# Masking the decay rows first, two visits for the gate products, and later key products in a hybrid decoder layer

## The chip, the cores and the metric

The kernel runs on one core of a Trainium2 chip. The metric is device time in microseconds (us) of one execution; lower is better. The core has a matrix engine (TensorE, PE in the profile, with its weight loads as PEld), a vector engine (VectorE, DVE), an engine for activation functions (ScalarE, ACT), a general engine (GpSimd, POOL) and one that here only issues transfers (SyncE, SP). Each engine takes its instructions in its own order and waits for the others by semaphores. Products land in PSUM, eight banks of 128 x 512 floats; all else lives in SBUF or, for longer, in DRAM.

## The reference

One layer of a decoder over 1024 tokens of width 1024, in float32, without a batch:

- x is normalised (RMSNorm), and one projection gives the columns of two mixers.
- Mixer A has four heads of width 128 with a gated delta rule. Queries, keys and values go through a causal convolution of four taps and SiLU; queries and keys are normalised. Each token and head has a step size beta and a log decay g.
- Mixer B is dilated window attention with eight heads of width 64.
- Both outputs go through a projection and are added to x; then comes a normalisation, a gated MLP of inner width 2816 with a convolution of three taps, and a last normalisation.

The part that matters here is the decays and the keys' products of mixer A. In the reference, with gc the running sum of g within a chunk:

```
diff = gc[..., :, None] - gc[..., None, :]
dec_incl = jnp.where(incl, jnp.exp(jnp.where(incl, diff, 0.0)), 0.0)
kk = jnp.einsum('nbhtd,nbhjd->nbhtj', kc, kc)
lmat = dec_strict * kk * bc[..., None, :]
attn = dec_incl * jnp.einsum('nbhtd,nbhjd->nbhtj', qc, kc) * bc[..., None, :]
```

So a head needs the matrix of decays exp(gc_t - gc_j) where t is not before j, and zero elsewhere. The kernel uses chunks of 128 tokens, eight of them (`NCH`).

## The kernel before

**The weave.** The order of work on PE is not written out by hand. Every part of the layer is a generator (`norms`, `gates`, `first`, `dense`, `kprep`, `qprep`, `vprep`, `merge`, `chain`, `attention`, `mlp_up`, ...), added to a planner `Weave` with a level. The planner keeps its own clock of PE and of each engine with a cost per operation; `Weave.run` always resumes the generator of lowest level among those that are due. A generator yields the time until it wants to be resumed: `yield wv.need(tiles, slack=s)` means "when these tiles are ready by the plan, and s us after". `next_bank(tag, *tiles, slack=0.0)` yields until the tiles are ready and a bank of that tag is free by the plan, and then takes the bank; each tag has two banks in turn. The order in which the products are emitted is binding for PE (`stamp_issue_order_token`), and the planner's times are only estimates: on the chip, PE waits wherever its next product's inputs or bank are not there. For the other engines the compiler's scheduler puts the operations in order, by its own estimates, within the dependencies; `after` adds an order between two operations of it.

**Dense products.** The projection's products are the stream that fills PE: `dense` goes over the columns in 128s, for each of them two halves of 512 tokens, and for each half eight times three products (`mm3`: a float32 product is made of three products of parts `hi` and `lo`). In the profile these are `ps<-xhi,wlo`, `ps<-xhi,whi` and `ps<-xlo,whi`. The text counts positions on PE in these dense products from the start of the program. The first three keys come from `first`, which runs while x is being loaded. The weights of a column are loaded to `wst` and split by ACT (`whi`) and DVE (`wlo`).

**Norms and gates.** `norms` sums the squares of x over the channels (eight small products with `ones`), makes `rst` with DVE and POOL, transposes it in two times four transposes into a PSUM bank each, and copies each to `rstdB`. `gates` makes the eight gate rows (beta and decay of four heads) by products of the weights `wba` with x: per half of the tokens eight products in two visits of four, `APART` (0.5 us) apart in the plan. Then come eight products with `sel` that bring the rows to tokens, elementwise work on DVE and ACT, and the running sum by two products with `tri`; the rows of sums go by DMA to DRAM (`gdram`).

**Key preparation, `kprep(h)`, one per head.** First the decay matrix `dec`: the head's rows of sums are loaded from `gdram` into all partitions, ACT subtracts the token's own sum chunk by chunk (eight Identity operations with the bias `ngc`), POOL's `affine_select` writes `NEG` (-1e30) where the mask is off, and ACT takes one Exp over 128 x 1024. A copy `gel` of the last columns is made by DVE before; it overlaps the same tile, so the eight operations on ACT come after it. Two `after` calls put these behind the head's convolution work. Then `tokens` transposes the key chunks: two banks of four transposes (`ps<-ident,kT`), copied to `ktok` by ACT, with eight Squares of 128 x 128 on ACT (`sq<-ps`) that sum the norm to `ssk`. From that DVE and POOL make the scales `nk`, `bp` and `ke`. Then two banks of four key products `ps<-kT` (keys with keys), each followed by four DVE operations `um<-ps,bp,dec` that scale and mask. The four transposes' banks and the products' banks are the same two, of tag `atr`; a product must wait until ACT's last Square has read the bank.

**After the keys.** `qprep(h)` starts when the head's key work is emitted: transposes (`ps<-ident,qT`), eight Squares on ACT, eight products (`ps<-qT,kT`) and eight DVE operations to `at`, in the same banks. `forward_sub` starts after the fourth head's keys; its blocks come through DRAM (`mdram`), DVE inverts, and `merge` builds the inverses by small products (`ps<-x,um` is the first of them) with copies such as `w2` between. Then come the chains over the chunks, attention, the output projection and the MLP, which takes most of the time.

Line numbers: products are recorded at L177, transposes at L181, all operations of ACT, DVE, POOL and the transfers of SP at L132. The work can so be told apart by tile names only.

Of the kernel before, what the change touches and what calls it, by code (L numbers as in the profile page):

```python
# [9 lines left out]
AF = mybir.ActivationFunctionType  # L10
OP = mybir.AluOpType
# [4 lines left out]
P = 128  # L16
# [3 lines left out]
NCH = 8  # L20
FT = 22
NEG = -1.0e30
APART = 0.5
EPS = 1e-6
SLOTS = {"kT": 2, "kU": 2, "dv": 2, "dw": 2, "kt": 4, "uy": 5, "qa": 4, "ev": 2, "go": 2, "Xa": 7, "Xb": 9}
TURNS = {"kT*": ("kT", "kU"), "dv*": ("dv", "dw"), "X": ("Xa",) * 7 + ("Xb",) * 9}
# [109 lines left out]
def hybrid_layer(tc, I, out):  # L136
    nc = tc.nc
    wv = Weave()
    ve = Engine(wv, nc.vector, "vector", 0.07, 0.00105)
    ac = Engine(wv, nc.scalar, "scalar", 0.12, 0.00085)  # L140
    po_ = Engine(wv, nc.gpsimd, "gpsimd", 0.15, 0.0021)
# [69 lines left out]
    def rsqrt(dst, src, n):  # L211
        po_.tensor_tensor(dst, src, mhalf[:, :n], op=OP.pow)
# [13 lines left out]
    def bank(tag, name="ps"):  # L226
        return tile_(pp_, (P, 512), F32, name, tag, 2)

    def next_bank(tag, *tiles, slack=0.0):

        while max(wv.need(*tiles), wv.slot_free(tag, 2)) + slack > 1e-3:
            yield max(wv.need(*tiles), wv.slot_free(tag, 2)) + slack
        return bank(tag)
# [4 lines left out]
    def v8(t):  # L238
        return t.rearrange("p (c t) -> p c t", c=NCH)
# [14 lines left out]
    for k in range(KT):  # L254
# [30 lines left out]
        else:  # L285
            inst = ve.tensor_tensor(acc, acc, sq, op=OP.add)
# [44 lines left out]
    rstdB = const("rstdB", [P, S])  # L331

    def norms():
        yield wv.need(acc, slack=8.0)
        ssp = yield from next_bank("atr", acc)
        for c in range(NCH):
            mm(ssp[:, c:c + 1], acc[:, c * P:(c + 1) * P], ones[:, :1], 0.215)
            if c % 2:
                yield APART
        ve.tensor_scalar(rst, ssp[:, :NCH], 1.0 / 1024, EPS, op0=OP.mult, op1=OP.add)  # L340
        rsqrt(rst, rst, NCH)
        wv.done.add("rst")
        yield wv.need(rst)
        for h in range(2):
            pb = yield from next_bank("atr")
            for c in range(4):
                i = 4 * h + c
                tp(pb[:, c * P:(c + 1) * P], rst[:, i:i + 1].to_broadcast([P, P]))
            ve.tensor_copy(rstdB[:, half(h)], pb)
        wv.done.add("norms")  # L350
# [4 lines left out]
    ngc = sp.tile([P, NCH, H], F32, name="ngc")  # L355

    def gates():

        yield wv.need(wba, xts[-1], slack=4.0)
        for h in range(2):  # L360
            pt = yield from next_bank("atr", wba, xts[-1])
            for k in range(KT):
                o = 32 * (k % 4)
                mm(pt[o:o + 32], wba[:, k, :], xts[k][:, half(h)], 0.23, k < 4, k >= 4, tile_position=(0, o))
                if k == 3:
                    yield APART
            ac.activation(barow[:, half(h)], pt, AF.Copy)
            yield APART
        yield wv.need(barow, slack=2.0)
        pt = yield from next_bank("atr", barow)  # L370
        for c in range(NCH):
            mm(pt[:, c * 8:(c + 1) * 8], barow[:, c * P:(c + 1) * P], sel, 0.215)
            if c % 2:
                yield APART
        yield from wv.until("rst")
        ba = sp.tile([P, NCH, 8], F32, name="ba")
        ve.tensor_tensor(ba, pt[:, :64].rearrange("p (c j) -> p c j", c=NCH),
                                rst[:, :, None].to_broadcast([P, NCH, 8]), op=OP.mult)
        ac.activation(beta, ba[:, :, :H], AF.Exp, scale=-1.0)
        ve.tensor_scalar(beta, beta, 1.0, None, op0=OP.add)  # L380
        ve.reciprocal(beta, beta)
        zt = sp.tile([P, NCH, H], F32, name="zt")
        ve.tensor_tensor(zt, ba[:, :, H:], dtb[:, None, :].to_broadcast([P, NCH, H]), op=OP.add)
        az = sp.tile([P, NCH, H], F32, name="az")
        ac.activation(az, zt, AF.Abs)
        ac.activation(az, az, AF.Exp, scale=-1.0)
        ac.activation(az, az, AF.Ln, bias=1.0)
        ve.scalar_tensor_tensor(az, zt, 0.0, az, op0=OP.max, op1=OP.add)
        ea = sp.tile([P, H], F32, name="ea")
        ac.activation(ea, alog, AF.Exp)  # L390
        g = sp.tile([P, NCH, H], F32, name="g")
        ve.scalar_tensor_tensor(g, az, -1.0, ea[:, None, :].to_broadcast([P, NCH, H]), op0=OP.mult,
                                       op1=OP.mult)
        pt = yield from next_bank("atr", g)
        g32 = g.rearrange("p c h -> p (c h)")
        mm(pt[:, :NCH * H], tri, g32, 0.215)
        mm(pt[:NCH * H, P:2 * P], g32, tri, 0.215)
        grow = tile_(sp, [NCH * H, P], F32, "grow", "osq", 1)
        ac.activation(grow, pt[:NCH * H, P:2 * P], AF.Copy)
        sy.dma_start(gdram, grow)  # L400
        ve.tensor_copy(gc, pt[:, :NCH * H].rearrange("p (c h) -> p c h", c=NCH))
        ve.tensor_scalar(ngc, gc, -1.0, None, op0=OP.mult)
        ac.activation(ngam, gc, AF.Exp)
        ve.tensor_scalar(ngam, ngam, -1.0, None, op0=OP.mult)
        wv.done.add("gates")
# [118 lines left out]
    def kprep(h):  # L524
        d = G[h]
        kT = T["k", h]
        yield from wv.until("gates")
        yield wv.need(gc)

        dec = A("dec", ("dv", "dw")[h % 2])  # L530
        gend = small("gend")
        gel = small("gel")
        rows = gdram.rearrange("(c h) t -> h c t", h=H)[h]
        sy.dma_start(v8(dec), bass.AP(tensor=rows.tensor, offset=rows.offset, ap=[[0, P]] + list(rows.ap)))
        late = "the rows may come later than the keys"
        after(ve.tensor_copy(gel, v8(dec)[:, :, P - 1]), kends[h][1], late)
        for c in range(NCH):
            inst = ac.activation(v8(dec)[:, c, :], v8(dec)[:, c, :], AF.Identity, bias=ngc[:, c, h:h + 1])
            after(inst, kends[h][0], late)
        po_.affine_select(v8(dec), v8(dec), pattern=[[0, NCH], [1, P]], compare_op=OP.is_ge, fill=NEG,  # L540
                                base=0, channel_multiplier=-1)
        ve.tensor_tensor(gend, gel, gc[:, :, h], op=OP.subtract)
        ac.activation(dec, dec, AF.Exp)
        eg = small("eg")
        ac.activation(eg, gend, AF.Exp)
        ge = small("ge", 4)
        ac.activation(ge, gel, AF.Exp)
        yield wv.need(kT, slack=SLACK)
        ssk = small("ssk")
        d["ktok"] = yield from tokens(kT, A("ktok", "kt"), None, ssk)  # L550
        ve.tensor_scalar(ssk, ssk, 4.0 * EPS, None, op0=OP.add)
        nk = small("nk", 4)
        po_.tensor_tensor(nk, ssk, phalf, op=OP.pow)
        bp = small("bp", 4)
        ve.reciprocal(bp, ssk)
        ve.tensor_tensor(bp, bp, beta[:, :, h], op=OP.mult)
        ke = small("ke", 4)
        ve.tensor_tensor(ke, bp, eg, op=OP.mult)

        um = A("um", "uy", shape=(P, NCH, P))  # L560
        for c0 in range(0, NCH, 4):
            pt = yield from next_bank("atr")
            for c in range(4):
                cs = slice((c0 + c) * P, (c0 + c + 1) * P)
                mm(pt[:, c * P:(c + 1) * P], kT[:, cs], kT[:, cs], 0.215)
            for c in range(4):
                i = c0 + c
                ve.scalar_tensor_tensor(um[:, i, :], pt[:, c * P:(c + 1) * P], bp[:, i:i + 1],
                                               dec[:, i * P:(i + 1) * P], op0=OP.mult, op1=OP.mult)
        md = mdram[h].rearrange("(c r) (j i) -> r j c i", r=4, j=32)  # L570
        for r in range(4):
            b = slice(32 * r, 32 * r + 32)
            sy.dma_start(md[r], um[b, :, b])
        d.update(kT=kT, dec=dec, ge=ge, nk=nk, bp=bp, ke=ke, um=um)
        wv.done.add(("k", h))
        if all(("k", i) in wv.done for i in range(H)):
            forward_sub()

    def qprep(h, qT):
# [4 lines left out]
        yield from tokens(qT, None, None, ssq)  # L584
        ve.tensor_scalar(ssq, ssq, 128.0, 128.0 * EPS, op0=OP.mult, op1=OP.add)
        rq = small("rq", 4)
# [143 lines left out]
    def chain(h):  # L730
# [62 lines left out]

        ve.tensor_scalar(ms, ms, 1.0 / 128, EPS, op0=OP.mult, op1=OP.add)
        rsqrt(ms, ms, NCH)
# [290 lines left out]
    def rms2_power():  # L1086
# [3 lines left out]
        rs = sp.tile([P, NCH], F32, name="rs")  # L1090
        ve.tensor_scalar(rs, ps[:, :NCH], 1.0 / 1024, EPS, op0=OP.mult, op1=OP.add)
        rsqrt(rs, rs, NCH)
# [393 lines left out]
```

## Time and profile before

| | us |
|---|---|
| median of 3 runs | 1257.34 |
| lowest and highest run | 1256.65, 1259.51 |
| the profiled execution's own time | 1259.56 |
| its span, first to last instruction | 1257.8 |
| PE busy (98% of the span) | 1233.0 |
| DVE busy (74%) | 936.0 |
| ACT busy (49%) | 621.8 |
| POOL busy (4%) | 47.8 |
| mean granted clock of TensorE | 0.993 |

The span is cut into stretches by the transfers and by the stage: the load of x and the first keys up to about 60 us, key preparation of the four heads between 60 and 115 us, queries, values and the merge up to about 240 us. In a line of the timeline, the first number is the start in us from the span's start, the second the duration of the group of instructions, then come the engine, the line, the operation, the tiles (out<-in), the shape and the number of instructions; in brackets stands how long the engine was idle before and which instruction released it. Matmuls are pipelined, so a group's duration reaches past the start of the next. A line of PE's waits gives what was waited for: total us, times, longest. A line of a table by windows gives the stretch, its length and then for each engine busy us and number of instructions; the last three numbers are the granted clock of PE, the share of the DMA engines and GB/s.

Not only idle time counts: at a granted clock of 0.50 a dense product starts every 0.43 us, and at 1.00 every 0.227 us.

### The profile page before, as it was taken

How to read it: one execution, taken by the hardware profiler on the slowest of the kernel's cores; microseconds unless marked ns; L12 is line 12 of the kernel's file. 1: busy time of each engine (PE TensorE's matmuls, PEld its weight loads, DVE VectorE, ACT ScalarE, POOL GpSimd, SP SyncE). 2: the span in 40 equal slices, each digit the busy share in tenths (PEclk: the TensorE clock that was granted, in tenths of full speed). 3: DMA queues.
4: the chain of work that ended last, by engine and by line, in shares of the span. 5: the costliest groups of instructions: out<-in, count | busy, mean ns of one | idle time of the engine just before them, and what ended most of it. 6: DMA issues, size and time to landing. Idle time of an engine off the chain costs nothing.

```text
span 1257.8 us, 18320 instructions
## 1 busy us (share of the span) xinstructions
PE 1233.0 (98%) x7040; PEld 1002.1 (80%) x7040; DVE 936.0 (74%) x1462; ACT 621.8 (49%) x1179; POOL 47.8 (4%) x34
## 2 busy tenths in 40 slices
PE   9989999999999999999999999999999999999996
PEld 7768887888676767878788888888888888787886
DVE  7566975563555455676798888888988989899875
ACT  7374444462757374465554454544544454343451
POOL 0021110022000000000000000000000000000000
PEclk9989999999999999999999999999999999999998
DMA  6313244255223420454312313223223298545523
GB/s 228 100 57 94 85 116 137 101 160 206 96 78 100 140 63 26 126 179 139 118 51 101 92 59 101 85 67 101 79 73 101 68 353 290 167 138 198 192 85 134
DMA packets 81974, 153.52 MB, mean 122 GB/s; under 512 B 21824, under 2 KB 32736, under 8 KB 81888
## 3 DMA queue, kind: packets, MB, share of 16 engines
q1 hardware_dynamic: 81888, 152.37, 37.1%
q8 instruction: 55, 0.90, 0.3%
q14 instruction: 31, 0.25, 0.1%
HBM read 114.31 MB, written 35.93 MB: 119 GB/s over the span
## 4 chain that ended last, share of the span: by engine, by line
PE 84%; DVE 7%; DMA 4%; ACT 2%; issue 2%; SPq 0%; POOL 0%; POOLq 0%; DVEq 0%; ACTq 0%
PE ps L177 44%; PE pa L177 18%; PE pc L177 9%; PE dw L177 8%; PE ps L181 4%; DMA wd<-in_wd 3%; DVE pr L132 2%; DVE x1h L132 1%; DVE wd L132 1%; ACT dec L132 1%; DVE kT L132 1%; PE warm L177 1%; DMA wst<-in_wu 0%; DVE r L132 0%; DVE xr L132 0%
## 5 line engine op out<-in xcount | busy, mean ns | idle before, releaser
L177 PE MATMUL dw<-pr 128*128 128x512 f32 (+1 forms) x984 | 213.3, 377 | 2.8 <-DVE x1h L132 2.8
L177 PEld LDWEIGHTS dw<-pr 128*128 128x128 f32 x984 | 176.1, 188 | 38.9 <-DVE x1h L132 4.9
L177 PE MATMUL ps<-xhi,whi 128*128 128x512 f32 x448 | 186.5, 416 | 0.0
L177 PE MATMUL ps<-xhi,wlo 128*128 128x512 f32 x448 | 175.8, 392 | 0.0
L177 PE MATMUL ps<-xlo,whi 128*128 128x512 f32 x448 | 175.3, 391 | 0.0
L177 PE MATMUL pa<-T,pair 128*128 128x512 f32 x528 | 127.1, 389 | 0.6 <-ACT u L132 0.6
L177 PEld LDWEIGHTS pa<-T,pair 128*128 128x128 f32 x528 | 99.0, 188 | 21.1 <-ACT u L132 0.7
L177 PEld LDWEIGHTS ps<-xhi,whi 128*128 128x128 f32 x448 | 84.6, 189 | 19.9 <-issue 6.0
L177 PEld LDWEIGHTS ps<-xhi,wlo 128*128 128x128 f32 x448 | 84.4, 188 | 18.5
L177 PEld LDWEIGHTS ps<-xlo,whi 128*128 128x128 f32 x448 | 84.8, 189 | 13.5
L132 ACT ACTIVATE sm<-sm,mx 128x512 f32<-128x512 f32 (+2 forms) x128 | 79.9, 651 | 23.0 <-DVE mx L132 23.0
L132 ACT ACTIVATE u<-pa 128x512 f32<-128x512 f32 x44 | 26.4, 600 | 110.5 <-PE pa L177 110.5
L132 DVE SCALAR_TENSOR_TENSOR y<-xu,fcw,y 128x1023 f32<-128x1023 f32 (+1 forms) x44 | 56.3, 1281 | 25.7 <-ACT y L132 25.7
L132 ACT ACTIVATE whi<-wst 128x1024 fp32r<-128x1024 f32 (+2 forms) x38 | 38.7, 1017 | 70.4 <-PE ps L177 63.0
L177 PE MATMUL pc<-B,pair 128*128 128x512 f32 x264 | 63.4, 389 | 0.0
L177 PE MATMUL pa<-B,A 128*128 128x512 f32 x264 | 63.4, 389 | 0.0
L177 PE MATMUL pc<-T,S 128*128 128x512 f32 x264 | 63.4, 389 | 0.0
L177 PE MATMUL pa<-T,S 128*128 128x512 f32 x264 | 63.4, 389 | 0.0
L132 ACT ACTIVATE pr<-wd 128x1024 fp32r<-128x1024 f32 x33 | 35.0, 1061 | 55.0 <-DVE wd L132 36.5
L132 DVE TENSOR_TENSOR wst<-wst 128x512 f32<-128x512 f32 x88 | 60.5, 687 | 0.7
L177 PE MATMUL ps<-B,pair 128*128 128x512 f32 x252 | 60.5, 389 | 0.0
L177 PEld LDWEIGHTS pc<-B,pair 128*128 128x128 f32 x264 | 49.6, 188 | 10.3
(230 smaller groups left out, 2279.8 us busy)
## 6 DMA issues: line engine op xcount, KB each, us to landing
wst<-in_wu SPq DMA_DIRECT2D x44, 512.0 KB, 3.7
wd<-in_wd SPq DMA_DIRECT2D x44, 512.0 KB, 4.3
wst<-in_wi SPq DMA_DIRECT2D x25, 512.0 KB, 3.7
upark<-y SPq DMA_DIRECT2D x22, 512.0 KB, 3.7
apark<-aqkv SPq DMA_DIRECT2D x12, 512.0 KB, 2.8
r<-upark SPq DMA_DIRECT2D x11, 512.0 KB, 7.6
r<-upark SPq DMA_DIRECT2D x22, 256.0 KB, 6.7
wa<-in_wd SPq DMA_DIRECT2D x22, 256.0 KB, 2.9
```

The lines of the kernel that those rows point to most:

```text
L132: return getattr(eng, op)(*a, **kw)
L177: tc.stamp_issue_order_token(nc.tensor.matmul(dst, lhs, rhs, start=start, stop=stop, **kw).ins, TOKEN)
L181: tc.stamp_issue_order_token(nc.tensor.transpose(dst, src, ident).ins, TOKEN)
```

## The change

Four edits are made.

1. In `kprep` the mask comes first: POOL's select runs on the loaded rows, and ACT's eight operations with the bias are Exp instead of Identity. The Exp over 128 x 1024 goes. Where the mask is off, Exp gets -1e30 plus the bias and gives zero.
2. In `gates` the eight products of a half are emitted in one visit, and the pause after is two `APART`.
3. In `norms` the second four transposes wait in the plan for the first copy to `rstdB`, plus 0.3 us.
4. In `kprep` the first bank of key products is asked for with a slack of `KSLACK`, 3 us in the plan.

The plan decides what follows from it on PE: the order of the transposes and products of the four heads changes between dense positions 78 and about 720.

```diff
+KSLACK = 3.0
...
         for h in range(2):
+            if h:
+                yield wv.need(rstdB, slack=0.3)
             pb = yield from next_bank("atr")
...
                 mm(pt[o:o + 32], wba[:, k, :], xts[k][:, half(h)], 0.23, k < 4, k >= 4, tile_position=(0, o))
-                if k == 3:
-                    yield APART
             ac.activation(barow[:, half(h)], pt, AF.Copy)
-            yield APART
+            yield 2 * APART
...
         sy.dma_start(v8(dec), bass.AP(tensor=rows.tensor, offset=rows.offset, ap=[[0, P]] + list(rows.ap)))
+        po_.affine_select(v8(dec), v8(dec), pattern=[[0, NCH], [1, P]], compare_op=OP.is_ge, fill=NEG,
+                                base=0, channel_multiplier=-1)
         late = "the rows may come later than the keys"
         after(ve.tensor_copy(gel, v8(dec)[:, :, P - 1]), kends[h][1], late)
         for c in range(NCH):
-            inst = ac.activation(v8(dec)[:, c, :], v8(dec)[:, c, :], AF.Identity, bias=ngc[:, c, h:h + 1])
+            inst = ac.activation(v8(dec)[:, c, :], v8(dec)[:, c, :], AF.Exp, bias=ngc[:, c, h:h + 1])
             after(inst, kends[h][0], late)
-        po_.affine_select(v8(dec), v8(dec), pattern=[[0, NCH], [1, P]], compare_op=OP.is_ge, fill=NEG,
-                                base=0, channel_multiplier=-1)
         ve.tensor_tensor(gend, gel, gc[:, :, h], op=OP.subtract)
-        ac.activation(dec, dec, AF.Exp)
...
         for c0 in range(0, NCH, 4):
-            pt = yield from next_bank("atr")
+            pt = yield from next_bank("atr", slack=KSLACK * (c0 == 0))
             for c in range(4):
                 cs = slice((c0 + c) * P, (c0 + c + 1) * P)
                 mm(pt[:, c * P:(c + 1) * P], kT[:, cs], kT[:, cs], 0.215)
```

## The prediction

> **What bounds the kernel now.** I read the page's busy line and its chain of waits first. TensorE (PE) is busy 1233.0 of 1257.8 us, and 84% of the chain that ended last is PE; so only time in which PE stands still, or runs at half clock, can be won, and every new stop of PE is paid in full.
>
> ```profile
> PE 1233.0 (98%) x7040; PEld 1002.1 (80%) x7040; DVE 936.0 (74%) x1462; ACT 621.8 (49%) x1179; POOL 47.8 (4%) x34
> PE 84%; DVE 7%; DMA 4%; ACT 2%; issue 2%; SPq 0%; POOL 0%; POOLq 0%; DVEq 0%; ACTq 0%
> ```
>
> Then PE's waits, by whom it waited for. The first line is the largest and lies in the stage that the change touches.
>
> ```profile
> PE ps L177 <- ACT sq L132: 5.0, 2, 4.4
> PE ps L177 <- DVE rstdB L132: 2.1, 1, 2.1
> PE ps L181 <- DVE rstdB L132: 0.8, 1, 0.8
> ```
>
> Then PE's timeline around those waits, with the clock by stretches (columns of the last two lines: busy us of PE and its weight loads, of DVE, ACT and POOL, then granted clock, DMA share, GB/s).
>
> ```profile
> 38.80 0.65 PE L181 MATMUL ps<-ident,rst 128*128 128x128 f32 x4 [0.78 <-DVE rstdB L132]
> 61.12 1.03 PE L181 MATMUL ps<-ident,kT 128*128 128x128 f32 x8
> 66.54 0.39 PE L177 MATMUL ps<-xhi,wlo 128*128 128x512 f32 x1
> 71.35 2.07 PE L177 MATMUL ps<-kT 128*128 128x128 f32 x8 [4.42 <-ACT sq L132]
> 75.78 1.66 PE L177 MATMUL ps<-kT 128*128 128x128 f32 x8
> 175.39 1.03 PE L181 MATMUL ps<-ident,qT 128*128 128x128 f32 x8
> 179.70 1.05 PE L177 MATMUL ps<-qT,kT 128*128 128x128 f32 x8
> ...
> 70.23:77.05 6.82, 5.70 (x20) 5.12 (x21) 5.20 (x9) 6.79 (x27) 2.70 (x2) 0.50 0.01 2
> 1244.42:1247.82 3.40, 1.30 (x12) 1.12 (x11) 2.94 (x8) 0.75 (x2) 0.00 (x0) 1.00 0.73 242
> ```
>
> To be seen: PE stands 4.42 us before the first head's key products (71.35), because their PSUM bank is still being read by ACT's squares, and the clock is 0.50 from 70.23 to 77.05. The reason is ACT's queue, which works in order:
>
> ```profile
> 60.33 2.46 ACT L132 ACTIVATE dec<-dec,ngc 128x128 f32<-128x128 f32 x8 [1.38 <-DVE gel L132]
> 67.04 0.27 ACT L132 ACTIVATE sq<-ps 128x128 f32<-128x128 f32 x1
> 67.29 1.06 ACT L132 ACTIVATE dec<-dec 128x1024 f32<-128x1024 f32 x1
> 68.23 0.27 ACT L132 ACTIVATE sq<-ps 128x128 f32<-128x128 f32 x1
> 68.49 2.46 ACT L132 ACTIVATE dec<-dec,ngc 128x128 f32<-128x128 f32 x8
> 70.93 0.28 ACT L132 ACTIVATE sq<-ps 128x128 f32<-128x128 f32 x1
> ```
>
> The fourth square of the first bank starts at 70.93 and the product follows 0.42 later. Between the squares stand the whole-row Exp of this head and the eight biased copies of the next.
>
> **Part 1, the decays.** Four Exps of 128x1024 go: 4 x 1.056 = 4.2 us of ACT. The eight copies with a bias become eight Exps with a bias; an Exp of that form isn't in the trace, so I bound it by the Identity's 0.392 us below and, above, by 1.056/8 more, 0.52; the operand form is the same, so I take 0.392. The four selects on POOL (1.10 each, POOL is 4% busy) come first: the rows are issued at 48.6 to 51.6 and land 5.5 to 8.4 later, the first Exp comes at 60.3, so select and row still fit ahead of it; if not, the gel copy on DVE, and the keys' convolution queued behind it, would come up to 1.1 late. By itself this part moves no PE instruction; it takes 1.06 and a wait on POOL out of the middle of the squares.
>
> **Part 2, gates and norms.** Ten visits to PE before and ten after, same products. The second four transposes of the norms come nine dense products later, so the 0.78 us wait goes. What else moves there I put between 0 and 0.6: 0.3. POOL's two short operations keep their order; the gates end some 3 us earlier, and with them the DMA of the rows on SP, which waits for nothing else of the change.
>
> **Part 3, the key products later.** From the instruction order of the two programs, positions counted in dense products on PE: the first head's transposes are at 189 in both; its key products were at 210 and 216 and are now all eight at 219. The second head's transposes were at 228 and 243, now 240 and 249; the other heads' transposes come at 252 to 276 instead of 270 to 297, their products at 294, 315, 336 in blocks of eight. The third head's query products, 15 dense products behind its transposes before, now follow them at once (576).
>
> I replay this with durations of the trace. PE reaches 189 at 61.12 - 0.78 - 0.3 - what the earlier gates give, some 59.7 to 60.0. Thirty dense products at 0.227 (63.82 to 64.05 and so on) and eight transposes (0.8 from 175.39 to 176.19) bring it to 219 at 67.4. ACT: its eight Exps end at 61.3, the steps to the first of the three squares left take 4.25 as before (62.79 to 67.04), then squares stand 0.40 apart (71.33 to 71.73): the last starts at 66.5, the bank is free at 66.9. The 4.42 is gone. But now the second half follows at once, and its bank's squares stand behind the eight Exps of the second head: 66.8 + 2.46 = 69.25, four squares, the last at 70.45, free at 70.87. PE is there at 68.1. **New wait: 2.75.** On PE everything dense is queued behind it.
>
> Next late: the third head's transposes need banks whose last squares wait, behind a Tanh of the fourth key and eight Exps, for DVE, which now does eight um products (0.344 each) in one go ahead of gel. I get 81.7 against PE's 80.4 and 85.96 against 84.33: 1.3 and 1.6; the bounds are 0 (before there was 0.57 in that stretch) and the 2.46 of eight Exps each.
>
> Third head's query: from the transposes at T, PE is ready at T + 0.79; ACT does a conversion (1.06), a square, the value's copy (1.15) and three squares, free at T + 3.44 (175.39 to 178.83). **New wait: 2.65.** SP's queue only has one weight load ahead of the four loads of x (3.27 for issuing all four) and two stores moved; nothing on PE waits for these. The merge's second product finds w2 some 0.8 late on DVE (bounds 0 and 1.12).
>
> Five visits fewer cut the dense stream; one costs 0.08 (176.19 to 176.50 against 0.227) to some 0.2: 0.7 in all.
>
> **The clock.** At 0.50 a dense product takes 0.43 (73.65 to 74.08). Before, two stretches of 3.41 us ran at half clock and lost 2.85 of work. The two drops of the clock, 70.23 and 1247.82, are 345 x 3.413 apart, so it is judged on a fixed grid: a stretch with 2.10 idle (1244.42 to 1247.82) was followed by 0.50; one with 1.1 idle (around 1153.71) was not. A wait of 2.7 puts at least 1.7 of idle into one stretch in about 8 of 10 positions, so I let both new waits halve the clock. One stretch costs 3.41 x (1 - 0.227/0.43) = 1.6, two 2.85; the stretch from 70.23, 2.25 busy, didn't give the clock back. I take 1.6 for the first, since PE's lateness is partly made up at the 1.3 wait, and 2.2 for the second.
>
> **Sum.** Gone: 4.42 + 0.57 + 0.78 + 2.85 + 0.7 + 0.3 = 9.6. New: 2.75 + 1.3 + 1.6 + 2.65 + 0.8 + 1.6 + 2.2 = 12.9. Net +3.3. The profiled execution took 1259.56 (span 1257.8), which would become 1262.9; it lies 2.2 above the median of the runs, 1257.34, on which I put the forecast: **1260.6**.
>
> **Rivals.**
> - A, as above: 1260.6, 1259 to 1262.5 by its halvings.
> - B, one of the two waits falls across the grid and keeps the clock: 1.9 less, 1258.7.
> - C, faster or the same: neither wait halves it. For it: 1.1 idle kept it; against it: 2.10 dropped it. The price is 3.8, so 1256.8; with the 1.3 and 1.6 at their lower bound 1253.9. It decides from an idle share above some 2.7 of 3.41. [...]
> - D, slower: DVE's blocks of eight um products, 2.75 each, hold both banks while the next transposes come; one um half late (1.12) at each of three heads adds 3.4: 1264. For it: DVE's queue is full at 77 to 82; against: 21 dense products (4.8 us) lie between most blocks.
> - E, faster: the 4.2 us less of ACT put it so far ahead that the squares are there first; the waits 2.75, 1.3, 1.6 and the first halving go, 7.25: 1253.4. It needs ACT 2.75 earlier at 70; but only 1.06 of the Exps lies ahead of that point.
>
> **Numbers.** A 0.46, B 0.12, C 0.24, D 0.10, E 0.08. A measurement of this kernel tells 0.2%, 2.5 us, from no change: slower is above 1259.86, faster below 1254.82. A gives 0.32 slower and 0.14 same; B 0.10 same, 0.02 slower; C 0.13 faster, 0.11 same; D 0.10 slower; E 0.08 faster. Faster 0.21, same 0.35, slower 0.44. The range 1254.5 to 1263.5 leaves out E, the lowest part of C, and most of D; A's own is 1259 to 1262.5.
>
> **What would show it.** In the changed kernel: no wait before the first four key products and about 2.75 on ACT's squares before the next four; waits of the third head's transposes on squares; about 2.65 at its query products; granted clock 0.50 after the first and after the third head's query; no wait of transposes on rstdB. I am wrong if the squares of the second bank come before the next head's Exps in time, or if the clock stays 1.00 after either wait.

## The result: slower by 0.43%

The changed kernel takes 1263.84 us (median of 10 runs, 1262.02 to 1266.85); the kernel before, in 10 runs beside it, 1259.32 (1256.65 to 1261.89). The ratio is 1.0043, 95% interval 1.0034 to 1.0051: 5.4 us slower, 4.3 to 6.4 (the medians alone differ by 4.5). The profiled execution took 1266.85 and is the slowest of the ten; its span is 1264.7, 6.9 longer than that of before.

The page of the changed kernel; its busy line and its chain hardly differ from before, so the loss must be looked for in waits:

```profile
PE 1235.4 (98%) x7040; PEld 1003.3 (79%) x7040; DVE 939.1 (74%) x1462; ACT 617.0 (49%) x1175; POOL 45.0 (4%) x34
...
PE 84%; DVE 7%; DMA 4%; ACT 3%; issue 2%; SPq 0%; POOLq 0%; DVEq 0%; POOL 0%; ACTq 0%
```

PE's waits after (lines are one further down, since a constant was added above). The 4.42 and the 0.78 of before are gone; other waits have come, in sum more. The largest:

```profile
PE ps L178 <- ACT sq L133: 5.1, 2, 2.7
PE ps L182 <- ACT sq L133: 2.5, 2, 1.5
...
PE ps L182 <- DVE gel L133: 1.7, 1, 1.7
PE ps L182 <- ACT ot L133: 1.4, 2, 0.8
PE ps L178 <- ACT w L133: 1.2, 2, 0.7
```

PE's timeline after, at the same places as before:

```profile
62.30 1.06 PE L182 MATMUL ps<-ident,kT 128*128 128x128 f32 x8 [1.74 <-DVE gel L133]
...
70.18 1.16 PE L178 MATMUL ps<-kT 128*128 128x128 f32 x8
74.07 1.28 PE L178 MATMUL ps<-kT 128*128 128x128 f32 x8 [2.73 <-ACT sq L133]
...
86.35 0.66 PE L182 MATMUL ps<-ident,kT 128*128 128x128 f32 x4 [1.04 <-ACT sq L133]
...
90.57 0.66 PE L182 MATMUL ps<-ident,kT 128*128 128x128 f32 x4 [1.48 <-ACT sq L133]
...
176.24 1.04 PE L182 MATMUL ps<-ident,qT 128*128 128x128 f32 x8
...
179.67 1.16 PE L178 MATMUL ps<-qT,kT 128*128 128x128 f32 x8 [2.40 <-ACT sq L133]
```

The first four key products (70.18) no longer wait; the next four do, 2.73, then two transposes, then the third query's products. These are the waits that the prediction listed. (The key of the transposes at 86.35 and 90.57, which the prediction calls the third head's, is that of the fourth, made by `dense`; it comes ahead of the third's.) What the first line shows was not listed: the first transposes wait 1.74 on DVE and start 1.2 later than before (61.12), where 1.1 to 1.4 earlier was expected.

The same work placed on both kernels' clocks shows where the 6.9 came from:

| start of | before | after | difference | by the prediction's sum |
|---|---|---|---|---|
| first key's transposes | 61.12 | 62.30 | +1.2 | -1.1 |
| first query's transposes | 124.60 | 125.48 | +0.9 | -2.4 |
| third query's transposes | 175.39 | 176.24 | +0.9 | -2.4 |
| first product of the MLP (`pa`) | 604.7 | 611.4 | +6.7 | +3.3 |

From the third query on, 5.8 was lost where 5.7 was expected, though not by the terms expected; ahead of it 3.3 went missing, 2.3 of that already at the first transposes and 1.0 between there and the third query's.

What DVE and POOL did there, in the changed kernel, from the timeline (a group's duration covers all its instructions):

```profile
51.50 1.10 POOL L133 TENSOR_SCALAR_AFFINE_SELECT dec<-dec 128x1024 f32<-128x1024 f32 x1 [14.29 <-DMA dec<-gdram]
51.52 0.68 DVE L133 TENSOR_TENSOR xr<-ps,rstdB 128x512 f32<-128x512 f32 x1
52.12 7.63 DVE L133 SCALAR_TENSOR_TENSOR kT<-xr,gcw,kT 128x1023 f32<-128x1023 f32 x4
...
53.34 1.28 POOL L133 TENSOR_SCALAR_AFFINE_SELECT dec<-dec 128x1024 f32<-128x1024 f32 x1 [0.74 <-DMA dec<-gdram]
55.19 3.48 POOL L133 TENSOR_SCALAR_AFFINE_SELECT dec<-dec 128x1024 f32<-128x1024 f32 x2 [0.57 <-DMA dec<-gdram]
```

and before, where the selects came at 62.86 and later:

```profile
52.94 4.86 DVE L132 SCALAR_TENSOR_TENSOR kT<-xr,gcw,kT 128x1023 f32<-128x1023 f32 x4
```

The same four convolution steps take 7.63 instead of 4.86 us while the four selects run beside them, and the last two selects take 3.48 together instead of 2.20, one of them 1.97. The multiplication at 51.52, which reads PSUM and one SBUF tile, keeps its 0.68 beside the select at 51.50 (the median of the 32 of its kind is 0.69 in both traces). The longest step is 2.10, that is 0.82 over its 1.28 and less than one select of 1.10. Why the two are slower beside each other, no trace shows.

### The profile page after: what moved, and what is told of

Read it like the earlier page. It is cut to its first block, busy times and chain, and to the rows that moved or that the text cites. A ratio compares the mean times of both kernels' runs of the same rounds, so it can differ in the third digit from the quotient of the medians.

```text
span 1264.7 us, 18306 instructions
## 1 busy us (share of the span) xinstructions
PE 1235.4 (98%) x7040; PEld 1003.3 (79%) x7040; DVE 939.1 (74%) x1462; ACT 617.0 (49%) x1175; POOL 45.0 (4%) x34
## 4 chain that ended last, share of the span: by engine, by line
PE 84%; DVE 7%; DMA 4%; ACT 3%; issue 2%; SPq 0%; POOLq 0%; DVEq 0%; POOL 0%; ACTq 0%
PE ps L178 44%; PE pa L178 19%; PE pc L178 9%; PE dw L178 8%; PE ps L182 3%; DMA wd<-in_wd 2%; DVE pr L133 2%; DVE x1h L133 1%; DVE kT L133 1%; DVE wd L133 1%; ACT dec L133 1%; PE warm L178 1%; ACT sq L133 1%; DVE r L133 1%; DMA mixer<-ot 0%
```

## The experiments

All ratios are to the kernel before, measured on the same chip, with 95% intervals.

### One part at a time

`only_mask`:

```diff
+        po_.affine_select(...)                       # ahead of gel and the eight operations
-        ... AF.Identity, bias=ngc ...
+        ... AF.Exp, bias=ngc ...
-        po_.affine_select(...)
-        ac.activation(dec, dec, AF.Exp)
```

> The kernel before with the mask first and the Exp with bias alone (no change of gates, norms or slack). Theory 1: the rows land some 3 us later than in the changed kernel, so fewer selects lie beside the first key's convolutions, but they still slow DVE by 1 to 2.8; the first products' wait on squares stays between 3 and 5; time 1259 to 1261. Rival (the selects do not slow DVE): ACT is 1.06 us shorter ahead of the first products, the wait falls to about 3.4, time 1258.2 or less. In this order the third query's products come nine dense products behind the transposes, with up to 1.3 us of wait.

Measured: 1262.62, ratio 1.0032 (1.0020 to 1.0044), so the mask first, with the order on PE that its plan gives, is a loss of 4 us by itself (2.5 to 5.5; 3.0 by the medians), above the range given. The first transposes start at 63.14 instead of 61.12, with 1.40 of wait on gel; a convolution step takes up to 2115 ns (before: 1285). The wait of the first products is 2.68, less than the 3 to 5 expected: PE comes 2.0 later, and the Exp of 1.06 no longer stands between the squares.

`only_gates`:

```diff
+            if h:
+                yield wv.need(rstdB, slack=0.3)
...
-                if k == 3:
-                    yield APART
...
-            yield APART
+            yield 2 * APART
```

> The kernel before with the edits of gates and norms alone. The wait of 0.78 on rstdB goes and the gates end 3 us earlier; the order from dense position 126 on is that of before. Theory: the selects stay behind the Identities as before, DVE's convolutions stay at 1.28 each, the wait of 4.42 stays between 4 and 5; time 0.5 to 1.4 lower than before, 1258.3. Rival (rows that land earlier pull other work of DVE or POOL into the convolutions): no gain, 1259.3 or more.

Measured: 1258.45, ratio 0.9991 (0.9982 to 0.9999). First transposes at 59.75, 1.4 earlier; the wait before the first products is 4.28. The selects lie at 61.38 and later, the convolutions take at most 1284 ns. Theory held.

`only_later`:

```diff
-            pt = yield from next_bank("atr")
+            pt = yield from next_bank("atr", slack=KSLACK * (c0 == 0))
```

> The kernel before with the slack of the key products alone. All eight key products of the first head stand at 225; I expect 1 to 1.5 us of wait before the first four and 2.5 to 3 before the next four, on ACT's squares; the first head's query products follow their transposes at 384 and wait 2.4 to 2.7; the third's do not. Theory (each wait is paid in full, halvings of the clock come in about half of the executions): 1259.5 to 1262. Rival (the later products win, the loss of the whole change comes from the selects alone): 1256 to 1258.

Measured: 1265.53, ratio 1.0046 (1.0031 to 1.0061). The waits in this order: 1.00 and 3.02 before the two halves of the first key products, 2.00 at a transpose, 1.32 and 1.34 at the first query's halves. The size is above the range given: in the profiled execution the clock stood at 0.50 in three places (77 to 80, 90 to 94, 131 to 138). In this trace, too, a convolution step beside a select is slow: the one at 71.98 took 2.12, beside the second head's select at 71.94.

`no_later`, the change without this part:

```diff
-KSLACK = 3.0
+KSLACK = 0.0
```

> The change without the slack of the key products: mask first and gates alone. The third query's products then stand at 585 and 591 and the key products at 207 and 210, with each head's between the transposes again. Theory (three causes: selects on DVE some 2 to 4 us, query wait 2.4 and more, new waits of keys): the selects' cost stays, the first products wait about 2.5, the wait at the query is under 0.5; time 1260 to 1262. Rival (the later keys are what costs, the mask first is a gain): 1257 to 1258.5.

Measured: 1261.62, ratio 1.0024 (1.0012 to 1.0036), in the range of the theory. First transposes at 61.99, with the same 1.7 on gel; key products wait 5.7 in three places, the third query's 0.3. So on top of the other parts the later keys cost some 2 us more (1.0043 against 1.0024, two intervals that just overlap); the parts do not add up to the whole (0.32 + 0.46 - 0.09 = 0.69%), since each plan orders PE anew.

### The selects beside the convolutions

`late_select`:

```diff
+        after(sel_, kends[h][0], late)               # sel_ is the select
```

> All of the change, but each head's select is held behind the Tanh of that head's key, so that it no longer runs beside the convolutions on DVE. Theory 1 (POOL's early selects slow DVE: the group of four convolutions from 52.12 took 7.63 against 4.86 us before): the group takes about 4.9 again, the 1.74 us wait of the first transposes goes or falls under 0.5, and the time falls by 1.5 to 2.7 from that of the changed kernel, to about 1261.5. The select now stands between gel and the Exps of its head, 1.1 each, so the wait on the second half's squares may grow by up to 1. Rival (DVE was slow for another reason, or the first transposes would wait anyway): the convolutions stay at 7.6, time 1263.8 or more. The waits of 2.73, 1.04, 1.48 and 2.40 stay under both.

Measured: 1263.07, ratio 1.0031 (1.0019 to 1.0042). The edit did not do what it was made for: `after` orders the compiler's plan, and it left no wait between these two engines, so on the chip three of the four selects still ran at 51.81, 53.63 and 55.48, and the fourth, which moved to 75.48, ran ahead of its Tanh, too (the four Tanhs start at 59.33, 66.47, 73.75 and 82.00). A convolution step still takes up to 2106 ns, the first transposes wait 1.27 instead of 1.74. It decides nothing on the cause, but it gives a pair on the clock, used below.

`no_select`, with the selects out of the way altogether:

```diff
-        po_.affine_select(v8(dec), v8(dec), ..., fill=NEG, ...)
...
-            ... AF.Exp, bias=ngc[:, c, h:h + 1])
+            ... AF.Exp, bias=gc[:, c, h:h + 1], scale=0.0)
```

> All of the change, but the four selects on POOL are left out, and with them the mask; so that the unmasked Exps stay bounded they take the token's own sum alone (scale 0). The decays and so the output are not the layer's. The order on every other engine is that of the changed kernel. Theory 1 (the selects slow DVE's first convolutions): the four convolutions take 1.28 each, 4.9 in all, the first transposes come at 59.7 to 60.6 without a wait on gel over 0.3; time 2 to 3 us under the changed kernel, 1261 to 1262. Rival: the convolutions still take 7.6, time 1263.8.

Measured: 1259.84, ratio 1.0010 (1.0001 to 1.0020): 4.2 us under the changed kernel (0.33%), more than the 2 to 3 expected. The convolution steps of this kernel (ns, smallest, median and largest):

```profile
L133 DVE SCALAR_TENSOR_TENSOR kT<-xr,gcw,kT x12: 1273/1276/1282, 49.9 to 76.3; 128x1023 f32<-128x1023 f32 x4, 128x1022 f32<-128x1022 f32 x4, 128x1021 f32<-128x1021 f32 x4
```

and its PE timeline:

```profile
60.00 1.03 PE L182 MATMUL ps<-ident,kT 128*128 128x128 f32 x8
...
70.89 1.16 PE L178 MATMUL ps<-kT 128*128 128x128 f32 x8 [2.15 <-ACT sq L133]
```

No step is over 1282 ns, and the first transposes start at 60.00, where the prediction's replay put them (59.7 to 60.0). PE's order was the same in all 7040 products. Nor did DVE wait for a select's result in the changed kernel: between 52 and 62 us it was idle only for ACT, 0.58, as here (0.59). So it is the selects that lengthen the steps. Of the 4.2, 2.3 are seen at the first transposes; 0.4 of these lie ahead of the selects, as the rows are issued at 45.41 here and at 45.80 in the changed kernel, which leaves 1.9. Another 0.6 is in the next wait (2.15 for 2.73). The rest was not separated; in this profiled execution the clock stayed 1.00 behind that wait, and it did not drop at 624 us, as it did in the changed kernel.

### The new waits

`q_spaced`:

```diff
-            pt = yield from next_bank("atr")         # in qprep
+            pt = yield from next_bank("atr", slack=3.0 * (h == 2 and c0 == 0))
```

> All of the change, but the third head's query products are asked for 3 us of plan later: all eight at 591 instead of 576 and 582. Theory 2: the wait of 2.40 and the half clock behind it go, 2.4 to 4 us: 1260 to 1261.5. Rival (what follows, merge and chains, waits for these products or for DVE in the same way, and the gain is given back): 1263 or more.

Measured: 1258.28, ratio 0.9992 (0.9983 to 1.0000): with this alone the changed kernel is no slower than before. 6.4 us went by the ratios (0.51%), 5.6 by the medians, where 2.4 to 4 were expected. The wait of 2.40 is gone and the clock stays 1.00 there; besides, the waits in the chains over the chunks changed. First after, then q_spaced, 240 to 400 us:

```profile
PE ps L182 <- ACT ot L133: 1.4, 2, 0.8
PE ps L178 <- ACT w L133: 1.2, 2, 0.7
PE ps L182 <- POOL vtok L133: 0.5, 1, 0.5
PE ps L178 <- DVE ct L133: 0.4, 1, 0.4
PE ps L178 <- ACT pb L133: 0.2, 1, 0.2
```

```profile
PE ps L178 <- ACT w L133: 1.6, 2, 1.2
PE ps L178 <- ACT pb L133: 0.2, 1, 0.2
```

3.7 against 1.8 (before: 2.0). So the sooner query products cost 2.4, some 1.6 of half clock and 1.9 in the chains. Why the chains suffer was not separated further: the order on PE differs between the two kernels from 180 to 298 us. Not all of the gain need come from the edit: ahead of it, where both kernels are the same, the four convolution steps took 6.76 us in this execution and the first transposes waited 0.89, not 7.63 and 1.74 (`exps_after`: 6.77 and 0.88). The cost of the selects so differs by some 0.9 between executions.

`exps_after`:

```diff
+        if h == 1:
+            yield from wv.until(("t", 0))
         for c in range(NCH):
             ...
+            if h == 1:
+                after(inst, sqends[0], late)         # the first head's last Square; same engine
```

> All of the change, but the eight Exps of the second head stand behind the first head's squares on ACT. Theory 2 (the second half of the first key products waits for squares that stand behind these Exps): the wait of 2.73 falls under 0.6, the clock stays 1.00 there, the waits of the third head's transposes grow by up to 1 each, as ACT's Exps come later; the select's cost of 1.7 and the wait of 2.40 stay; time 1260 to 1262.5. Rival (the wait only moves to the next bank): 1263.8.

Measured: 1264.13, ratio 1.0032 (1.0020 to 1.0045). The wait of 2.73 became 0.66 and 0.44 for the two halves, but a transpose of the fourth key now waits 2.74 instead of 1.04, and the half clock moved there with it (84 to 88). That is the rival: the Exps of this one head now stood in the way of the next bank.

`squares_ahead`: from `only_gates`, the order on ACT for all heads and spaced products, with the decays in the old form.

```diff
+KSLACK = (4.0, 3.0, 2.0, 2.0)
+BSLACK = (0.5, 0.5, 0.5, 0.5)
...
+        if h in (1, 2, 3):
+            yield from wv.until(("t", h - 1))
...
+            if h in (1, 2, 3):
+                after(inst, sqends[h - 1], late)     # Identities behind the Squares of the head before
...
-        ac.activation(dec, dec, AF.Exp)
+        if h:
+            ac.activation(dec, dec, AF.Exp)
...
+        if h == 0:
+            after(ac.activation(dec, dec, AF.Exp), sqends[0], late)
...
+            pt = yield from next_bank("atr", slack=KSLACK[h] if c0 == 0 else BSLACK[h])
...
+            pt = yield from next_bank("atr", slack=2.0 * (h == 2 and c0 == 0))     # in qprep
```

> The kernel before with the edits of gates and norms, the decays as before (Identity, select, Exp), and on ACT the decays of a head put behind the squares of the head before, the first head's whole-row Exp behind its own squares; key products at 219, 264, 318, 336 by slacks per head, third query products at 600. Theory 2: the first products wait for at most 0.7, all key preparation together for at most 2.5, no half clock before the end; time 1253.5 to 1256. Rival (ACT as a whole is too slow in this stage, order does not matter): the waits move to the second and third head and the time is that of the gates' edits alone, 1258.5 or more.

Measured: 1251.50 (1251.05 to 1252.43), ratio 0.9943 (0.9931 to 0.9955), faster than both kernels and 2 us below the range given. All waits of PE between 26 and 120 us are this one line, and the clock stays 1.00 there:

```profile
PE ps L183 <- ACT sq L134: 1.3, 2, 0.7
```

ACT's queue in it, around the first key's squares:

```profile
66.71 0.28 ACT L134 ACTIVATE sq<-ps 128x128 f32<-128x128 f32 x1
...
68.31 0.28 ACT L134 ACTIVATE sq<-ps 128x128 f32<-128x128 f32 x1
...
68.58 1.05 ACT L134 ACTIVATE dec<-dec 128x1024 f32<-128x1024 f32 x1
69.52 2.44 ACT L134 ACTIVATE dec<-dec,ngc 128x128 f32<-128x128 f32 x8
```

The squares run through, and the decays follow in time for DVE. ACT does as much work as before (620.3 us against 621.8).

`slacks_only`, the same without the order on ACT:

```diff
-        if h in (1, 2, 3):
-            yield from wv.until(("t", h - 1))
...
-                after(inst, sqends[h - 1], late)
```

> The kernel squares_ahead without its order on ACT: gates' edits, decays as before, the same slacks for key and query products; in this plan the first key products stand at 228. Theory 2 (order on ACT is what counts, later products alone only move the wait): under 1 us before the first four products and 2 to 3 before the next four, waits of the later heads' transposes of 1 to 2 each; time 1255.5 to 1259. Rival (later positions alone do it): 1251.5 to 1253.5.

Measured: 1258.71, ratio 0.9993 (0.9984 to 1.0002). Waits of 3.0 before the second half of the first key products and 2.2 at a transpose, half clock behind both (74 to 77, 88 to 91). So the gain of `squares_ahead`, 6.3 us over this kernel by the ratios, needs ACT's order; placing the products later only moves the wait. The two differ in the order on PE, too (first key products at 219 and 228), which was not separated.

`ahead_mask`, `squares_ahead` with the mask first:

```diff
-KSLACK = (4.0, 3.0, 2.0, 2.0)
+KSLACK = (4.0, 3.0, 1.0, 1.0)
...
+        po_.affine_select(...)                       # first, as in the change
-        ... AF.Identity, bias=ngc ...
+        ... AF.Exp, bias=ngc ...
```

> The kernel squares_ahead with the mask first and the Exps with bias in place of Identity, select and Exp, slacks of 1 for the last two heads so that the queries stay where they were. Theory 1: the selects again run at 51 to 59 and slow the first key's convolutions by over 2 us, the first transposes wait about 1 on DVE; the 4.2 us that ACT saves buy nothing, as ACT no longer is waited for: 1253.5 to 1255.5. Rival (the shorter ACT work is worth more than the selects cost): 1251 or less.

Measured: 1257.72, ratio 0.9990 (0.9981 to 1.0000), 5.9 us above `squares_ahead` (0.47%), more than the 2 to 4 expected. Its waits from 26 to 120 us:

```profile
PE ps L183 <- DVE kT L134: 3.0, 1, 3.0
PE ps L183 <- DVE gel L134: 1.7, 1, 1.7
PE ps L179 <- ACT sq L134: 0.8, 2, 0.4
```

The 1.7 on gel is the selects' again. The 3.0 is new: with the long Exp gone from its costs, the plan asks for the next heads' transposes earlier (255 to 282 instead of 273 to 288), before DVE has made the key.

## Why the prediction was wrong, step by step

It said slower, and the waits on squares that it listed came; but it gave 3.3 us instead of 5.4, and the time, 1263.84, lies 0.3 above its range. It missed the first cost on the way, that of the selects.

- **The step that failed** is in part 1: "The four selects on POOL (1.10 each, POOL is 4% busy) come first", costed at nothing, because "by itself this part moves no PE instruction". The cover that it named was POOL's idle time; but the selects slowed DVE, which was on the way to the first key: 2.77 us on the convolutions, 1.9 to 2.3 at the first transposes, some 4 in the whole time (`no_select`, `only_mask`). What it did allow for, a select that is not done before the first Exp, did not happen: the last select ended at 58.67 and the first Exp started at 62.27. The trace of before had the sign: of its four selects, the one at 71.02, beside a convolution, took 1.40, and the others 1.09 to 1.10. I read that row only for its median.

```profile
L132 POOL TENSOR_SCALAR_AFFINE_SELECT dec<-dec x4: 1089/1099/1395, 62.9 to 84.0; 128x1024 f32<-128x1024 f32 x4
71.02 1.40 POOL L132 TENSOR_SCALAR_AFFINE_SELECT dec<-dec 128x1024 f32<-128x1024 f32 x1 [7.05 <-ACT dec L132]
68.86 2.60 DVE L132 SCALAR_TENSOR_TENSOR kT<-xr,gcw,kT 128x1022 f32<-128x1022 f32 x2
```

- **The base of the forecast.** The forecast was set on the median of three runs, 1257.34. Ten runs gave 1259.32, close to the profiled execution, 1259.56. The sum on that execution, 1262.9, was 0.9 under the median after. That is closer than the sum deserves: between the two profiled executions it was 3.3 for a measured 6.9. And the step above alone does not account for the number: with the forecast 2.0 higher, on 1259.32, the range would have held 1263.84, selects or not.
- **The new wait of 2.75:** measured 2.73. The replay from ACT's queue was right.
- **1.3 and 1.6 at the next key's transposes:** 1.04 and 1.48. Between the first transposes and the third query's the kernel won 0.3 where the sum has 1.3, although the waits there were 0.4 less than put (5.25 for 5.65). So 1.4 is missing in the other terms of that stretch, the fewer visits (0.7) and the clock (2.85 and 1.6); the runs do not separate them.
- **2.65 at the third query:** 2.40. What followed from it was not w2 on DVE (0.8 was put there) but 1.9 in the chains, which the prediction did not see. That the whole from the third query on came out right, 5.8 for 5.7, is luck: 0.8 for w2 and 0.6 too much for the clock stand in for the chains.
- **Part 2, 0.78 + 0.3:** `only_gates` shows 1.4 at the first transposes, and 1.1 us (0.1 to 2.3) in the time.
- **The clock, both waits halve it:** in the profiled execution both did, for one stretch of 3.41 each; the stretches around the waits are these (those behind the waits are cut 0.2 too early, hence 0.53; from 74.97 and 180.78 it is 0.50):

```profile
71.34:74.07 2.73, 0.00 (x1) 0.01 (x1) 2.69 (x4) 2.61 (x14) 0.00 (x0) 1.00 0.00 0
74.75:78.16 3.41, 3.41 (x13) 2.73 (x12) 3.38 (x11) 0.71 (x2) 1.27 (x1) 0.53 0.00 0
177.27:179.67 2.40, 0.01 (x1) 0.00 (x0) 2.30 (x2) 2.30 (x10) 0.00 (x0) 1.00 0.81 280
180.58:183.99 3.41, 3.41 (x14) 2.83 (x13) 3.04 (x8) 1.07 (x5) 2.89 (x3) 0.53 0.71 173
```

  The two drops, at 74.97 and 180.78, are 105.81 or 31 x 3.413 apart, the grid of the prediction. So 1.6 each was right, and 2.2 for the second too much. A third such stretch, from 624.51, is not in the sum and not in the trace of before; ahead of it 16 products of one column (1.84 us from 622.30 on) fall into one stretch of the grid, which has 0.34 idle, and in the trace of before into two. That these dropped the clock is not shown, and it did not drop so in every execution: over the ten runs the mean clock was 0.992 to 0.996, and the two with 0.992 took 1266.0 and 1266.9, the three with 0.996 1262.0 to 1263.0. In `late_select` a wait of the same 2.73 left it at 1.00. Its clock dropped at 177.78, 32 x 3.413 after 68.56, so the wait there lies across two stretches of the grid, with 1.14 and 1.58 idle, while its wait at the third query lies in one, with 2.23 idle:

```profile
70.82:73.55 2.73, 0.01 (x1) 0.00 (x0) 2.69 (x4) 2.62 (x14) 0.00 (x0) 1.00 0.05 14
68.56:71.97 3.41, 2.27 (x13) 1.56 (x12) 3.41 (x6) 3.35 (x17) 0.00 (x0) 1.00 0.51 159
71.97:75.38 3.41, 1.83 (x12) 1.71 (x13) 3.27 (x10) 2.53 (x11) 1.50 (x1) 1.00 0.00 0
174.37:177.78 3.41, 1.18 (x10) 0.85 (x8) 2.89 (x4) 3.23 (x10) 0.00 (x0) 1.00 0.82 322
177.78:181.19 3.41, 3.25 (x12) 2.96 (x13) 2.78 (x8) 1.59 (x10) 2.27 (x3) 0.50 0.79 195
```

  On the grid of each trace's own drops (before and after from 20 us to the end, the experiments but `only_mask`, `late_select` and `squares_ahead` from 27 to 259), every stretch at full clock with 1.95 us or more of PE idle (3.30 at most) was followed by 0.50, and none with 1.68 or less was, but for the one of after from 621.10, with the one-column products; in between lie one of 1.90 that dropped it (`no_later`) and one of 1.91 that did not (`exps_after`).

- **Rival C** (neither wait halves the clock): both waits, 2.73 and 2.40, were followed by 0.50 in the profiled execution. The stretches of 3.41 ahead of the two drops have 2.51 and 2.30 of PE idle, less than the 2.7 that C needs. In `late_select` 2.73 of wait, spread over two stretches with 1.14 and 1.58 idle, left the clock at 1.00; so in these traces the drops went with the idle time in one stretch, not with the length of the wait.
- **Rival D** (DVE's blocks of `um` hold the banks): no wait of PE is on `um` in the changed kernel. That its time, 1264, is close to the measured one is chance.
- **Rival E** (ACT's 4.2 us less win): the waits on the squares stayed. `squares_ahead` against `slacks_only` shows that ACT's order was worth some 6 us with no less work on it.

## What to carry to other kernels

Before an operation moves to an engine that is idle, look at what the other engines do at the new time: an engine's idle share says nothing on that. Here POOL was 4% busy, and beside its selects of 1.10 us DVE's steps of 1.28 took up to 2.10. The largest duration of a small group of like instructions, beside its median, showed the collision in the trace of before (1.395 for 1.099). And where products wait for an engine's queue, as here for squares of ACT that stood behind eight Exps, look first for what stands between the operations that free the bank. Moving the products later only carried the wait to the next bank (3.0 and 2.2 in `slacks_only`), while moving the other work behind those operations, for every head at once, removed nearly all of it (1.3 left in `squares_ahead`).

## What the runs showed that was not expected

- In the changed kernel POOL's selects of 128 x 1024 and DVE's convolution steps, which read two SBUF tiles, were slower beside each other: steps of 1.28 took up to 2.10, selects of 1.10 up to 1.97; one DVE multiplication beside a select, with one input from PSUM, kept its 0.68. Without the selects (`no_select`) no step took over 1.282.
- A wait of PE of 2.40 us, 2.30 of it within one stretch of the grid, was followed by half clock for a stretch of 3.41; another of 2.73, across two with 1.14 and 1.58 idle (`late_select`), was not. The ten executions of the changed kernel differ by 4.8 us, and the slowest have the lowest mean clock.
- In `late_select` an order between two engines, given to the compiler alone, did not hold on the chip: all four selects ran 6.5 us or more before the operation that they were to follow.
